# Moving cache copies, a table load and buffer choices in a hybrid decoder step

## The chip, the cores and the metric

The kernel runs on one core of a Trainium2 chip. The metric is the device time of one execution in microseconds (us); the time before is the median of three runs. The engines are named as in the profile: PE is TensorE (its matmuls; PEld its weight loads), DVE is VectorE, ACT is ScalarE, POOL is GpSimd and SP is SyncE. Each engine works through its own list of instructions in order, and transfers (DMAs) are issued from the lists of POOL and SP. "L936" is line 936 of the kernel before.

## The reference

One layer of a decoder is computed for 512 prompt tokens and for 8 samples of 4 tokens each, 544 columns in all. Cut to what matters:

```python
# mixer, for prompt and samples alike
q_a, k_a, v_a, r_a, z_a, q_b, k_b, v_b = split(rmsnorm(h) @ w_in)        # 2048 -> 6160
o_a, state = gla_recurrence(q_a, k_a, v_a, gate(z_a), state_gla)         # 10 heads, linear attention
o_a = rmsnorm(o_a) * silu(r_a)
o_b = dilated_attention(rope(q_b), concat(k_hist, rope(k_b)), concat(v_hist, v_b))   # 12 heads
h = h + concat(o_a, o_b) @ w_out
k_sample, v_sample = k_all[:, -1024:], v_all[:, -1024:]                  # the caches, moved on by 4 rows
# ConvFFN
up = rmsnorm(h) @ w_up                                                   # 2048 -> 2 x 5504
u, g = conv_b + causal_conv3(concat(conv_state, up), conv_w)
h = h + (silu(g) * u) @ w_down
y = rmsnorm(h)
```

Outputs are `y`, the linear-attention states, the new caches of the samples (1020 old rows and 4 new ones for each sample, for keys and for values) and the new convolution states.

## The kernel before

Activations stand with features on the 128 partitions and the 544 tokens along them, in two halves of 272 columns. Every large product is made of three matmuls in a reduced format: the high part of the weights with the high and the low part of the activations, and the low part of the weights with the high part. A weight unit is 8 x 128 rows by 128 columns, 512 KB: SP loads it into `raw` (three buffers), ACT writes its rounded high part `whi` (L190), and DVE the rest, `wlo` (L191), with three buffers each. A framework orders the instructions of each engine when the kernel is built, by its own estimates of time and by priorities (weight units are put far ahead), and adds the semaphores. A pool of buffers that takes over the memory of earlier pools waits until all of them are released.

The stages, in order: the q, k, v products of attention and its scores (to about 480 us); five blocks of linear attention, t = 0 to 4, each for two heads (`gla`, called at L818; the decay products E, KB, QB at L662 to L669, the scores on PE at L673), beside the input products that are left (to about 843 us); the output projection `w_out`, 16 tiles (loop from L928, to about 1061 us); the up-projection with convolution, 43 pairs of tiles (class Pair, to about 1985 us); the down-projection, first the three kept tiles (KEPT), then three groups (to the end).

What the change touches:

- **The caches' copies.** Sixteen copies (8 samples, keys and values; `kept_rows`), each from DRAM to DRAM and 3060 KB, issued on POOL's queue by `keep_rows` (L634). `keep_in_program_order` pins each behind the POOL instruction that the code issues before it. Two are issued in each block of linear attention, behind the store of the prompt's state (L738) and behind that of the samples' state (L773): ten. The other six are issued in the w_out loop at odd tiles (L945).
- **The split outputs.** Behind linear attention the 16 outputs `o` are split into high and low parts `ah`, `al` in the order 10 to 15, 0 to 9 (L869). Output k takes the pair of buffers k (`act_pair(k)`), which before held tile k of the normed input, read by the last input product.
- **The entry to the up-projection.** The pool FP opens when the pool HX of the w_out loop is closed. From it come the table `vcv` of the convolution's factors (172 KB, L1086) and the old convolution states `ci` (64 KB for four pairs, L1101), both loaded by POOL. ACT puts `ci` into the tiles F (L1028), later splits weights (L190) and copies a product from PSUM to `V` (L1038), and PE's next product into that PSUM buffer waits for this copy. The new states are gathered in `co`.
- **w_out.** For each tile POOL loads the old residual `h` from `xT` (L935), DVE adds the product (L936), and the sum is stored to `hscr` (L937).
- **Down-projection.** During the kept products, NSLOT = 11 tiles of the FFN's activations are fetched (`fetch`, SP into `ar`, two buffers, then split to `dh`, `dl`); the pool DS2 has 24 - NSLOT more. In the first group the stored residual is loaded into `hr`, one buffer of its own (L1201).

Of the kernel before, what the change touches and what calls it, by code (L numbers as in the profile page):

```python
# [9 lines left out]
F32 = mybir.dt.float32  # L10
# [7 lines left out]
P = 128  # L18
# [3 lines left out]
NB = 8  # L22
TS = 4
NS = NB * TS
NT = TP + NS
# [10 lines left out]
KF = FF // P  # L36
# [6 lines left out]
GATES_FIRST = 4  # L43
POOL_SPLIT = 6
NKEPT = 3
NSLOT = 11
FW = 2 + TP + NB * (2 + TS)


# [59 lines left out]
V_MIX, V_FFN, V_FIN, V_BG, V_GN, V_CW, V_CB = 0, 16, 32, 48, 53, 54, 54 + 258  # L109
NVEC = 54 + 258 + 86  # L110
# [13 lines left out]
def _build(tc, nc, es, xT, st_gla, ck, cv, conv_in, vecs, w_in, w_gu, w_out, w_up, w_dn,  # L124
# [123 lines left out]
    def act_pair(k):  # L248
        return (acts.tile([P, NT], F32R, tag=f"ah{k}", name=f"ah{k}"),
                acts.tile([P, NT], F32R, tag=f"al{k}", name=f"al{k}"))  # L250
# [378 lines left out]
    kept_rows = [(b, src, dst) for b in range(NB) for src, dst in ((ck, k_s), (cv, v_s))]  # L629

    def keep_rows():

        b, src, dst = kept_rows.pop(0)
        tc.keep_in_program_order(nc.gpsimd.dma_start(dst[b, 0:PAST - TS, :], src[b, TS:PAST, :]))  # L634
# [169 lines left out]
    for t in range(GP):  # L804
        q = scaled(in_tile(C_QA + t * P), "q", 0.125)
        k = scaled(in_tile(C_KA + t * P), "k")
        V = GL.tile([P, 4, 2 * P], F32, tag="V", name="V", bufs=2)
        Vs = GL.tile([NS, 2 * P], F32, tag="Vs", name="Vs", bufs=2)
        for e in range(2):
            v = scaled(in_tile(C_VA + (2 * t + e) * P), "v")  # L810
            pst = vps()
            for c in range(4):
                nc.tensor.transpose(pst[:, c * P:(c + 1) * P], v[:, c * P:(c + 1) * P], ident)
            nc.scalar.activation(V[:, :, e * P:(e + 1) * P], pst.rearrange("p (c v) -> p c v", c=4), AF.Copy)
            pst = vps()
            nc.tensor.transpose(pst[:NS, :P], v[:, TP:], ident)
            nc.scalar.activation(Vs[:, e * P:(e + 1) * P], pst[:NS, :P], AF.Copy)
        gla(t, q, k, V, Vs)  # L818
    for h in range(GATES_FIRST, 2 * GP):
        r = scaled(in_tile(C_RA + h * P), "r", -1.0)  # L820
        silu_neg(r)
        nc.vector.tensor_mul(o[h], o[h], r)
# [4 lines left out]
    wu_p, wu = opened(name="wu", bufs=1, side="right")  # L827
# [38 lines left out]

    order = [10, 11, 12, 13, 14, 15, 0, 1, 2, 3, 4, 5, 6, 7, 8, 9]
    og = [None] * KD
    for k in order:  # L869
        og[k] = act_pair(k)  # L870
        split(og[k][0], og[k][1], o[k])
    closed(rb2, rowsB_p, rowsA_p)

# [21 lines left out]
    def factors(some, X, pool):  # L895
# [24 lines left out]
        for i in some:  # L920
# [3 lines left out]
            else:  # L924
                parts(i, T3, 2, b[i][:, 1:3])

    X = {}
    for ot in range(KD):  # L928
        ps = gps()
        gemm(ps, [wpart(w_out, order[:8], ot * P), wpart(w_out, order[8:], ot * P)], og)  # L930
        i, j = divmod(ot, 2)
        if j == 0:
            hp = HX.tile([P, 2, NT], F32, tag="h", name="h", bufs=KD // 2 + 1 - AHEAD)
        ht = hp[:, j]
        nc.gpsimd.dma_start(ht, xT[ot * P:(ot + 1) * P, :])  # L935
        nc.vector.tensor_add(hv(ht), hv(ht), ps[:, :, :HT])  # L936
        nc.gpsimd.dma_start(hscr[ot], ht)  # L937
        if ot == 0:
            nc.scalar.activation(acc2, ht, AF.Square)
        else:  # L940
            sq = htmp("sq")
            nc.scalar.activation(sq, ht, AF.Square)
            nc.vector.tensor_add(acc2, acc2, sq)
        X[i] = hp
        if ot % 2 == 1 and kept_rows:  # L945
            keep_rows()
        nc.scalar.activation(ht, ht, AF.Copy, scale=vec[:, V_FFN + ot:V_FFN + ot + 1])
        if j == 1 and i < AHEAD:
            factors([i], X, VA)
# [27 lines left out]
    class Pair:  # L977
# [79 lines left out]
        def conv(self):  # L1057
            out = []
            for s, F in ((0, self.Fu), (1, self.Fg)):
# [19 lines left out]
    fp_p, FP = opened(name="ffn", bufs=1, side="right")  # L1079
# [2 lines left out]
    nc.scalar.activation(rstdF[:, 2:2 + TP], rstd[:, :TP], AF.Copy)  # L1082
    nc.scalar.activation(rstdF[:, 2 + TP:].rearrange("p (b s) -> p b s", s=2 + TS)[:, :, 2:],
                         rstd[:, TP:].rearrange("p (b t) -> p b t", t=TS), AF.Copy)
    vcv = FP.tile([P, NVEC - V_CW], F32, name="vcv")
    nc.gpsimd.dma_start(vcv, vecs[:, V_CW:])  # L1086

    ci_v = conv_in.rearrange("p (s f) r -> p s f r", s=2)
    co_v = conv_out.rearrange("p (s f) r -> p s f r", s=2)
    def sv(x):  # L1090
        return x[:, 2 + TP:].rearrange("p (b s) -> p b s", s=2 + TS)[:, :, :TS]

    KEPT = list(range(KF - 1 - NKEPT, KF - 1))
    kept = {}
    ci = co = None
    for f, pr in enumerate(pairs):
        if f % 4 == 0:
            n = min(4, KF - f)
            ci = FP.tile([P, 2, 4, 2 * NB], F32, tag="ci", name="ci", bufs=2)
            co = FP.tile([P, 2, 4, 2 + 2 * NB], F32, tag="co", name="co", bufs=2)  # L1100
            nc.gpsimd.dma_start(ci[:, :, :n, :], ci_v[:, :, f:f + n, :])  # L1101
        pr.ci, pr.co = ci[:, :, f % 4, :], co[:, :, f % 4, :]
        if f:
            pr.p5()
        pr.p6()
        pr.p2()
        pr.p7()
        if f + 1 < KF:
            pairs[f + 1].p1()
        pr.p3()  # L1110
        pr.p4()
        cu, cg = pr.conv()
        nc.scalar.activation(cg[:, :FW - 2], cg[:, :FW - 2], AF.Silu)
        a = FP.tile([P, NT], F32, tag="a", name="a", bufs=1)
        nc.vector.tensor_mul(a[:, :TP], cu[:, :TP], cg[:, :TP])
        nc.vector.tensor_mul(a[:, TP:].rearrange("p (b t) -> p b t", t=TS), sv(cu), sv(cg))
        if f in KEPT:
            kept[f] = (G0.tile([P, NT], F32R, tag="dh", name="dh"), G0.tile([P, NT], F32R, tag="dl", name="dl"))
            split(kept[f][0], kept[f][1], a)
        else:  # L1120
            nc.gpsimd.dma_start(adr[f], a)
        if f % 4 == 3 or f == KF - 1:
            f4 = f - f % 4
            nc.gpsimd.dma_start(co_v[:, :, f4:f + 1, :], co[:, :, :f + 1 - f4, :])
# [3 lines left out]
    rows_p, rows = opened(name="rows", bufs=KD)  # L1128
    ds_p, DS = opened(name="ds", bufs=NSLOT)

# [18 lines left out]
    with tc.high_priority(offset=min(1500, tc.cur_priority - P0)):  # L1149
        for k in groups[0][:NSLOT]:  # L1150
            A1[k] = fetch(k, 0)
# [7 lines left out]
    w3_p, W3 = opened(name="w3", bufs=1, side="right")  # L1159
# [8 lines left out]
    def ctile(name):  # L1168
        return W3.tile([P, NT], F32, tag="c", name=name, bufs=2)
# [20 lines left out]
    for gi, ks in enumerate(groups):  # L1190
        A = {}
        with tc.high_priority(offset=min(2000, tc.cur_priority - P0)):
            for k in ks:
                A[k] = A1[k] if k in A1 else fetch(k, where[k])
        if gi < len(groups) - 1:
            for ot in range(KD):
                ps = gps()
                gemm(ps, [wpart(w_dn, ks[i:i + 8], ot * P) for i in range(0, len(ks), 8)], A)
                nc.vector.tensor_add(hv(h[ot]), hv(h[ot]), ps[:, :, :HT])
                if gi == 0:  # L1200
                    x = W3.tile([P, NT], F32, tag="hr", name="hr", bufs=1)  # L1201
                    nc.sync.dma_start(x, hscr[ot])
                    nc.vector.tensor_add(h[ot], h[ot], x)

# [117 lines left out]
```

## Time and profile before

| | |
|---|---|
| runs of the kernel before | 2522.66, 2524.89, 2529.08 us |
| median | 2524.89 us |
| profiled execution, its own time | 2525.1 us |
| its span in the profile | 2523.3 us |
| mean granted clock of PE | 0.991 of full |
| busy, share of the span | PE 98%, DVE 64%, ACT 43%, POOL 17% |

The rows below come from this one profiled execution; its times count from the start of the span. A row of a timeline gives the start and the length of an instruction or a run of like ones; what stands in brackets is the idle time of its engine before it and what ended that. The granted clock is told in shares of full speed (2.4 GHz).

### The profile page before, as it was taken

Reading aid. Unit: us, or ns where it says so; the run is one execution under the profiler, and the core shown is the slowest. Engines: PE = TensorE matmul, PEld = TensorE weight load, DVE = VectorE, ACT = ScalarE, POOL = GpSimd, SP = SyncE. Lnnn points to the kernel's source line nnn. Section 1 sums busy time; section 2 is a strip of 40 time slices with the busy share of each in tenths; the row PEclk is TensorE's granted clock in tenths of the full one; section 3 lists DMA queues with packets and bytes.
Section 4 is the critical chain, followed back from the end, with each engine's and each line's share of the span. In section 5 each row is a group of like instructions: output and inputs, shape, how many; then the busy total and the mean of one; then the engine's idle time right before and its main releaser. Section 6 shows DMA issues by size and latency. Waiting matters only on the chain.

```text
span 2523.3 us, 47163 instructions
## 1 busy us (share of the span) xinstructions
PE 2462.7 (98%) x19479; PEld 2385.2 (95%) x19479; DVE 1619.3 (64%) x2460; ACT 1078.8 (43%) x1870; POOL 435.3 (17%) x581
## 2 busy tenths in 40 slices
PE   8999999999999899989999999999999999999997
PEld 8988887899999899989999999999999999999997
DVE  7777764267777843478878888888888643342243
ACT  6344464133334433355555555555555531131142
POOL 1333434210002320112212221222121000000001
PEclk9999999999999999999999999999999999999999
DMA  7777744544555498668888888889888473443232
GB/s 220 197 202 197 193 114 138 161 131 141 166 177 177 159 305 256 169 146 192 192 188 192 191 191 189 191 191 192 189 191 178 124 219 107 115 151 92 85 100 72
DMA packets 581593, 427.73 MB, mean 170 GB/s; under 512 B 18976, under 2 KB 553728, under 8 KB 580608
## 3 DMA queue, kind: packets, MB, share of 16 engines
q1 hardware_dynamic: 462144, 248.31, 34.9%
q0 software_dynamic: 115200, 171.02, 30.1%
q10 hardware_dynamic: 4032, 5.38, 0.6%
q8 instruction: 153, 2.51, 0.4%
q14 instruction: 64, 0.52, 0.1%
HBM read 397.40 MB, written 77.37 MB: 188 GB/s over the span
## 4 chain that ended last, share of the span: by engine, by line
PE 82%; DMA 8%; DVE 6%; issue 2%; POOL 1%; ACT 1%; SPq 0%; DVEq 0%; POOLq 0%; ACTq 0%
PE g L225 40%; PE b L965 20%; PE g L965 15%; DMA q<-qscr 6%; DVE pr L411 1%; PE v L507 1%; PE s L673 1%; DMA ar<-adr 1%; DVE wlo L191 1%; DVE kv L412 1%; PE s L561 1%; DMA xr<-in_xT_dram 0%; PE s L548 0%; PE s L795 0%; POOL q L408 0%
## 5 line engine op out<-in xcount | busy, mean ns | idle before, releaser
L191 DVE TENSOR_TENSOR wlo<-raw,whi 128x1024 fp32r<-128x1024 f32 (+1 forms) x341 | 408.3, 1198 | 295.6 <-ACT whi L190 288.7
L190 ACT ACTIVATE whi<-raw 128x1024 fp32r<-128x1024 f32 (+1 forms) x345 | 355.0, 1030 | 555.1 <-PE g L225 454.0
L225 PE MATMUL g<-ah,whi 128*128 128x272 f32 x2048 | 442.9, 296 | 9.8 <-ACT ah L190 4.6
L225 PE MATMUL g<-al,whi 128*128 128x272 f32 x2048 | 447.2, 297 | 0.5 <-DVE al L191 0.5
L225 PE MATMUL g<-ah,wlo 128*128 128x272 f32 x2048 | 442.4, 295 | 0.3 <-DVE wlo L191 0.3
L965 PE MATMUL b<-vh,whi 128*128 128x272 f32 x1376 | 395.1, 288 | 6.2 <-ACT V L1038 4.8
L965 PE MATMUL b<-vl,whi 128*128 128x272 f32 x1376 | 395.9, 289 | 0.8 <-DVE vl L893 0.6
L965 PE MATMUL b<-vh,wlo 128*128 128x272 f32 x1376 | 389.9, 288 | 1.3 <-DVE wlo L191 1.3
L225 PEld LDWEIGHTS g<-ah,whi 128*128 128x128 f32 x2048 | 327.9, 191 | 19.7 <-issue 10.3
L225 PEld LDWEIGHTS g<-al,whi 128*128 128x128 f32 x2048 | 329.2, 191 | 11.6 <-issue 9.3
L225 PEld LDWEIGHTS g<-ah,wlo 128*128 128x128 f32 x2048 | 328.3, 190 | 10.2 <-issue 8.5
L965 PE MATMUL g<-vl,whi 128*128 128x272 f32 x1032 | 298.8, 290 | 2.0 <-DVE vl L893 1.9
L965 PE MATMUL g<-vh,whi 128*128 128x272 f32 x1032 | 297.8, 289 | 0.4 <-ACT vh L892 0.3
L965 PE MATMUL g<-vh,wlo 128*128 128x272 f32 x1032 | 296.8, 288 | 0.0
L965 PEld LDWEIGHTS b<-vh,whi 128*128 128x128 f32 x1376 | 260.0, 189 | 6.7 <-ACT V L1038 5.1
L225 PE MATMUL g<-dh,whi 128*128 128x272 f32 x1248 | 258.0, 288 | 4.1 <-ACT whi L190 2.7
L965 PEld LDWEIGHTS b<-vl,whi 128*128 128x128 f32 x1376 | 259.5, 189 | 1.5 <-DVE vl L893 1.5
L965 PEld LDWEIGHTS b<-vh,wlo 128*128 128x128 f32 x1376 | 257.4, 189 | 1.5 <-DVE wlo L191 1.5
L225 PE MATMUL g<-dh,wlo 128*128 128x272 f32 x1248 | 258.2, 288 | 0.0
L225 PE MATMUL g<-dl,whi 128*128 128x272 f32 x1248 | 258.1, 288 | 0.0
L190 ACT ACTIVATE whi<-rs 128x1024 fp32r<-128x1024 f32 x129 | 136.8, 1061 | 266.8 <-PE g L965 201.1
L225 PEld LDWEIGHTS g<-dh,whi 128*128 128x128 f32 x1248 | 195.7, 188 | 5.4 <-ACT whi L190 3.4
(341 smaller groups left out, 4101.5 us busy)
## 6 DMA issues: line engine op xcount, KB each, us to landing
raw<-in_w_up_dram SPq DMA_DIRECT2D x129, 512.0 KB, 4.1
raw<-in_w_in_dram SPq DMA_DIRECT2D x96, 512.0 KB, 4.8
raw<-in_w_dn_dram SPq DMA_DIRECT2D x64, 512.0 KB, 4.0
out_k_s_dram<-in_ck_dram POOLq DMA_DIRECT2D x8, 3060.0 KB, 12.7
out_v_s_dram<-in_cv_dram POOLq DMA_DIRECT2D x8, 3060.0 KB, 14.5
ra<-in_w_up_dram SPq DMA_DIRECT2D x43, 512.0 KB, 7.9
rs<-in_w_up_dram SPq DMA_DIRECT2D x43, 512.0 KB, 3.8
rs<-in_w_up_dram POOLq DMA_DIRECT2D x43, 512.0 KB, 9.8
```

The lines of the kernel that those rows point to most:

```text
L190: nc.scalar.activation(hi, src, AF.Copy)
L191: eng.tensor_sub(lo, src, hi.bitcast(F32))
L225: nc.tensor.matmul(ps[:, s, :HT], a, b[:, s * HT:(s + 1) * HT], start=(i == 0 and n == 0), stop=(i == len(todo) - 1 and n == 2))
L411: nc.vector.tensor_mul(pr, kt[:, 4:5, :].broadcast_to([P, TS, QC]), q5[:, 1:5, :])
L412: nc.vector.tensor_mul(kt[:, 0:4, :], kt[:, 0:4, :], q5[:, 0:1, :].broadcast_to([P, 4, QC]))
L507: nc.tensor.matmul(psv[32 * m:32 * m + 32, :QC], lhs, rhs, start=(kt == 0), stop=(kt == 5), tile_position=(0, 32 * m))
L561: nc.tensor.matmul(psc[r, :P], vt[:, j * P + 64 * e:j * P + 64 * e + 64], t[:, j * P:(j + 1) * P], start=(j == 0), stop=(j == qi))
L673: nc.tensor.matmul(ps[:, c * P:(c + 1) * P], KS[:, c * P:(c + 1) * P], Q[:, :, c * 64:(c + 1) * 64], start=True, stop=True)
L965: nc.tensor.matmul(b[:, :HT], a_[:, i, :], x_[i][:, v, :], start=(first and i == 0 and n == 0), stop=(i == 7 and n == 2), skip_group_check ...
```

## The change

It has four parts.

1. `keep_rows()` is called a third time per block, after `gla(t)`. With that, 15 of the 16 copies are issued beside linear attention and the last at tile 0 of the w_out loop, where the condition on odd tiles is dropped.
2. The split outputs take the buffer pairs by their place in the order, `act_pair(n)`: output 10 the first pair, output 9 the last.
3. `vcv` and the buffers `ci` and `co` come from the pool `wu`, which opens before the w_out loop, instead of FP. `vcv` and the first `ci` are loaded by POOL before that loop; the later `ci` where they were. `wu` is 3552 bytes a partition larger.
4. NSLOT is 10 instead of 11 (so DS2 has 14 pairs instead of 13), and `hr` is taken from the two rotating buffers "c" of the down-projection.

```diff
--- before.py
+++ after.py
@@ -43,7 +43,7 @@
 GATES_FIRST = 4
 POOL_SPLIT = 6
 NKEPT = 3
-NSLOT = 11
+NSLOT = 10
 FW = 2 + TP + NB * (2 + TS)
 
 
@@ -816,6 +816,7 @@
             nc.tensor.transpose(pst[:NS, :P], v[:, TP:], ident)
             nc.scalar.activation(Vs[:, e * P:(e + 1) * P], pst[:NS, :P], AF.Copy)
         gla(t, q, k, V, Vs)
+        keep_rows()
     for h in range(GATES_FIRST, 2 * GP):
         r = scaled(in_tile(C_RA + h * P), "r", -1.0)
         silu_neg(r)
@@ -866,8 +867,8 @@
 
     order = [10, 11, 12, 13, 14, 15, 0, 1, 2, 3, 4, 5, 6, 7, 8, 9]
     og = [None] * KD
-    for k in order:
-        og[k] = act_pair(k)
+    for n, k in enumerate(order):
+        og[k] = act_pair(n)
         split(og[k][0], og[k][1], o[k])
     closed(rb2, rowsB_p, rowsA_p)
 
@@ -924,6 +925,21 @@
             else:
                 parts(i, T3, 2, b[i][:, 1:3])
 
+    vcv = wu.tile([P, NVEC - V_CW], F32, name="vcv")
+    nc.gpsimd.dma_start(vcv, vecs[:, V_CW:])
+    ci_v = conv_in.rearrange("p (s f) r -> p s f r", s=2)
+    co_v = conv_out.rearrange("p (s f) r -> p s f r", s=2)
+
+    def states(f):
+
+        n = min(4, KF - f)
+        ci = wu.tile([P, 2, 4, 2 * NB], F32, tag="ci", name="ci", bufs=2)
+        co = wu.tile([P, 2, 4, 2 + 2 * NB], F32, tag="co", name="co", bufs=2)
+        nc.gpsimd.dma_start(ci[:, :, :n, :], ci_v[:, :, f:f + n, :])
+        return ci, co
+
+    state = states(0)
+
     X = {}
     for ot in range(KD):
         ps = gps()
@@ -942,7 +958,7 @@
             nc.scalar.activation(sq, ht, AF.Square)
             nc.vector.tensor_add(acc2, acc2, sq)
         X[i] = hp
-        if ot % 2 == 1 and kept_rows:
+        if kept_rows:
             keep_rows()
         nc.scalar.activation(ht, ht, AF.Copy, scale=vec[:, V_FFN + ot:V_FFN + ot + 1])
         if j == 1 and i < AHEAD:
@@ -1082,23 +1098,15 @@
     nc.scalar.activation(rstdF[:, 2:2 + TP], rstd[:, :TP], AF.Copy)
     nc.scalar.activation(rstdF[:, 2 + TP:].rearrange("p (b s) -> p b s", s=2 + TS)[:, :, 2:],
                          rstd[:, TP:].rearrange("p (b t) -> p b t", t=TS), AF.Copy)
-    vcv = FP.tile([P, NVEC - V_CW], F32, name="vcv")
-    nc.gpsimd.dma_start(vcv, vecs[:, V_CW:])
-
-    ci_v = conv_in.rearrange("p (s f) r -> p s f r", s=2)
-    co_v = conv_out.rearrange("p (s f) r -> p s f r", s=2)
+
     def sv(x):
         return x[:, 2 + TP:].rearrange("p (b s) -> p b s", s=2 + TS)[:, :, :TS]
 
     KEPT = list(range(KF - 1 - NKEPT, KF - 1))
     kept = {}
-    ci = co = None
     for f, pr in enumerate(pairs):
         if f % 4 == 0:
-            n = min(4, KF - f)
-            ci = FP.tile([P, 2, 4, 2 * NB], F32, tag="ci", name="ci", bufs=2)
-            co = FP.tile([P, 2, 4, 2 + 2 * NB], F32, tag="co", name="co", bufs=2)
-            nc.gpsimd.dma_start(ci[:, :, :n, :], ci_v[:, :, f:f + n, :])
+            ci, co = states(f) if f else state
         pr.ci, pr.co = ci[:, :, f % 4, :], co[:, :, f % 4, :]
         if f:
             pr.p5()
@@ -1198,7 +1206,7 @@
                 gemm(ps, [wpart(w_dn, ks[i:i + 8], ot * P) for i in range(0, len(ks), 8)], A)
                 nc.vector.tensor_add(hv(h[ot]), hv(h[ot]), ps[:, :, :HT])
                 if gi == 0:
-                    x = W3.tile([P, NT], F32, tag="hr", name="hr", bufs=1)
+                    x = ctile("hr")
                     nc.sync.dma_start(x, hscr[ot])
                     nc.vector.tensor_add(h[ot], h[ot], x)
 
```

## Rows read from the trace of the kernel before

**Rows 1.** Windows: us, busy us of PE, PEld, DVE, ACT, POOL; PE clock, DMA, GB/s.

```profile
700.00:780.00 80.00, 80.00 (x672) 75.45 (x672) 56.92 (x104) 30.12 (x50) 9.39 (x10) 1.00 0.56 177
780.00:880.00 100.00, 93.84 (x734) 87.53 (x732) 84.03 (x135) 50.99 (x87) 30.64 (x20) 0.98 0.52 168
800.00:820.00 20.00, 20.00 (x164) 19.98 (x163) 19.75 (x37) 10.95 (x16) 5.52 (x3) 1.00 0.19 54
880.00:1060.00 180.00, 175.30 (x1358) 175.11 (x1358) 75.13 (x100) 60.48 (x81) 23.51 (x39) 0.97 0.81 245
...
870.00:880.00 10.00, 7.01 (x53) 6.39 (x51) 7.18 (x14) 4.34 (x9) 0.00 (x0) 0.94 0.99 345
...
1096.00:1101.00 5.00, 4.88 (x22) 4.56 (x22) 3.58 (x6) 1.21 (x4) 0.00 (x0) 0.53 1.19 209
2040.00:2480.00 440.00, 440.00 (x3518) 440.00 (x3517) 159.10 (x185) 114.78 (x139) 0.00 (x0) 1.00 0.38 111
```

**Rows 2.** Waits of PE, whole run: waited for, us in total, times, longest us.

```profile
PE b L965 <- ACT V L1038: 4.8, 1, 4.8
PE g L225 <- ACT ah L190: 4.6, 1, 4.6
```

**Rows 3.** Timeline of ACT and PE at the entry to the up-projection.

```profile
1089.02 0.21 ACT L1083 ACTIVATE rstdF<-rstd 128x32 f32<-128x32 f32 x1
1094.00 0.32 ACT L1028 ACTIVATE F<-ci 128x16 f32<-128x16 f32 x2 [4.77 <-DMA ci<-in_conv_in_dram]
...
1095.17 0.38 ACT L1038 ACTIVATE V<-b 128x272 f32<-128x272 f32 x1
...
1095.60 0.60 PE L965 MATMUL b<-vh,whi 128*128 128x272 f32 x1 [4.85 <-ACT V L1038]
```

**Rows 4.** Timeline of the DMA issues of POOL and SP.

```profile
777.40 0.54 POOL L634 DMA_DIRECT2D out_v_s_dram<-in_cv_dram  x1
...
778.65 0.37 SPq L209 DMA_DIRECT2D raw<-in_w_in_dram  x1
...
865.65 0.54 POOL L634 DMA_DIRECT2D out_v_s_dram<-in_cv_dram  x1
883.48 4.31 POOL L935 DMA_DIRECT2D h<-in_xT_dram  x8 [17.29 <-issue]
...
1088.35 0.59 POOL L1086 DMA_DIRECT2D vcv<-in_vecs_dram  x1 [2.01 <-DVE rstd L171]
1088.92 0.73 POOL L1101 DMA_DIRECT2D ci<-in_conv_in_dram  x1
```

**Rows 5.** Timeline of PE at the entry to w_out.

```profile
889.82 0.79 PE L225 MATMUL g<-ah,whi 128*128 128x272 f32 x2 [3.14 <-DVE h L936]
```

**Rows 6.** DMAs issued at 655, 777, 778 and 883 us: KB, us to landing.

```profile
raw<-in_w_in_dram SPq DMA_DIRECT2D x1, 512.0 KB, 4.1
...
out_v_s_dram<-in_cv_dram POOLq DMA_DIRECT2D x1, 3060.0 KB, 15.9
...
raw<-in_w_in_dram SPq DMA_DIRECT2D x1, 512.0 KB, 18.0
...
h<-in_xT_dram POOLq DMA_DIRECT2D x1, 272.0 KB, 5.4
```

**Rows 7.** The page's groups: busy us, mean ns, idle before them.

```profile
L225 PE MATMUL g<-al,whi 128*128 128x272 f32 x2048 | 447.2, 297 | 0.5 <-DVE al L191 0.5
```

**Rows 8.** Timeline of ACT behind the kept products.

```profile
2023.81 0.66 ACT L190 ACTIVATE dh<-ar 128x544 fp32r<-128x544 f32 x1 [1.28 <-DMA ar<-adr]
```

**Rows 9.** Timeline of ACT, DVE and PE in linear attention's last block.

```profile
800.38 1.06 ACT L190 ACTIVATE whi<-raw 128x1024 fp32r<-128x1024 f32 x1 [1.66 <-PE g L225]
801.47 1.44 DVE L191 TENSOR_TENSOR wlo<-raw,whi 128x1024 fp32r<-128x1024 f32 x1
...
810.08 0.85 DVE L669 TENSOR_TENSOR QB<-q,E 64x256 f32<-64x256 f32 x2
810.10 2.04 PE L673 MATMUL s<-QB,KB 128*128 128x128 f32 x16
```

## The prediction, made before the change was run

> **What bounds the kernel now.** The windows by stage come first: TensorE (PE) is busy for all of 80 us beside linear attention, for 440 of 440 us in the down-projection, and loses time in few places: 6.2 us in 780 to 880 us and 4.7 us in 880 to 1060 us [rows 1]. So an edit pays only if it shortens one of PE's own gaps, and costs only if it opens a new one. PE's waits come second: the longest is 4.8 us on V (L1038), then 4.6 us on ah [rows 2]. The instructions around those gaps come third. In the first, ACT is done at 1089.23 us (1089.02 plus 0.21), sits 4.77 us for the conv state `ci`, and only then reaches V, on which PE waits 4.85 us [rows 3]; `ci` was issued as late as 1088.92 us, behind the table `vcv` on POOL's queue [rows 4]. The second and third lie at the start of w_out: PE waits 4.6 us for the last split of the linear-attention outputs [rows 2] and, up to 889.82 us, 3.14 us for `h` [rows 5], whose load POOL issued at 883.48 us [rows 4], with 5.4 us to landing [rows 6]. After a gap PE doesn't run at the full 2.4 GHz at once: in 1096 to 1101 us the granted clock is 0.53, half, and 22 matmuls start in 5 us [rows 1]. At full clock one starts every 440/3518 = 0.125 us, so 22 take 2.75 us, and 2.2 us are lost beside the gap itself.
>
> **The early table and conv state.** Issued before the w_out loop, `vcv` and `ci` land some 200 us before ACT asks. ACT then does its L1028 at 1089.2 us, the weight split behind it, and V as soon as its product ends on PE, 1095.60 - 4.85 = 1090.75 us. V's start to PE's restart is 1095.60 - 1095.17 = 0.43 us [rows 3], so PE goes on at about 1091.4 us with some 0.2 us for the order on ACT: 4.2 us saved, and with so short a gap the 2.2 us of half clock too, **-6.4 us**. Bounds: -4 us if the half clock stays, -7.5 us if the rest of the gap goes as well. The two loads now stand on POOL's queue ahead of the `h` load. They cost it 0.59 and 0.73 us of issue [rows 4], but POOL idles 17.29 us before that load [rows 4], so they lie under that idle time; if POOL could not start them before 883.48 us, `h` would come 1.3 us later. The larger `wu` pool (3552 bytes a partition) moves no work; it is paid for below.
>
> **The freed buffers.** The split outputs now take activation buffers in the order in which the last input product frees them. PE's own waits on `al` in the whole run are 0.5 us [rows 7], and the 4.6 us gap ends with the split `ah` of the last linear-attention outputs, which are late because their values are [rows 2]: a buffer that is free earlier doesn't bring them. I take **-0.5 us**, bounds +3 us (another order of splits on DVE) and -3 us.
>
> **Room.** Ten slots instead of eleven: the eleventh prefetched tile is split on ACT at 2023.81 us after a wait for its own `ar` load [rows 8], behind the kept products, and the stage after it keeps PE at 440 of 440 us [rows 1]. `hr` goes into a rotating pair of buffers with two tenants instead of one of its own; the add that needs it is on DVE, busy for 159 of 440 us there [rows 1]. **0**, bounds -2 and +2 us.
>
> **Copies leave w_out.** PE's lost 4.7 us in 880 to 1060 us are the 3.14 us gap and the tail of the one before it [rows 1, 2, 5]; behind them it is always busy although five more copies run there. Taking those out gives PE nothing: **0**. Bounds: 0, and -1 us for a shorter tail of the half clock.
>
> **Copies beside linear attention.** This is the part that decides. Each copy is 3060 KB [rows 6]. While one runs, DMA is 0.99 busy at 345 GB/s (870 to 880 us) [rows 1], so it takes 3060/345 = 9 us in which there is no room. A copy issued at 777.40 us lands after 15.9 us, at 793.3 us, and the weight load issued at 778.65 us takes 18.0 us, landing at 796.65 us; away from a copy one takes 4.1 us [rows 4, 6]. A weight load beside a copy thus waits until the copy is through. The third copy of a block is pinned on POOL behind the second, with nothing of POOL between, so it is issued about 0.55 us after it and runs directly behind. The weight load then lands 9 us later.
>
> The Trainium skill, "DMA: Bandwidth & Descriptors", the paragraph on arbitration, says that a DMA engine alternates between the queues that have work and drains a whole packet of one before it turns to the next; that speaks against this change, since copies with long packets would take most of the time whatever stands in the other queue. The trace agrees as far as 18.0 us beside a copy against 4.1 us without go [rows 6]. Were the two served by bytes instead, the load would land early, and the sum would be that of the second case below.
>
> What the 9 us do differs by block. In blocks 0 to 2 (the stretch 700 to 780 us stands for them) DVE is busy 56.92 of 80 us and PE idles nowhere, beside two copies [rows 1]: a weight part that is late by a few us is made up. I take **+1 us** for the three, bounds 0 and +6 us. The third copy behind block 3 (at 777.95 us) meets the start of block 4. The load landing at 796.65 us is split at 800.38 us, so 3.7 us of lateness are free; with its landing at 805.7 us the split is 5.3 us late, and `wlo`, at 801.47 us on DVE, with it [rows 9]. Behind `wlo` DVE has the decay products up to QB at 810.08 us, with DVE busy 19.75 of 20 us [rows 1], so nothing is made up; PE starts the scores from QB within 0.02 us of QB's start [rows 9], so it stands still some 5.2 us, and 2.2 us of half clock follow: **+7.4 us**. Bounds: 0, if the loads issued ahead are split in another order or PE has products to put in, and +10 us.
>
> Block 4's own third copy is issued at 865.65 + 0.55 = 866.2 us [rows 4] and runs when the second is through, to about 889 us. The `h` load is behind it on POOL's queue: 883.48 + 5.4 = 888.9 us becomes between 890 (272 KB at 345 GB/s, behind 889) and 894.6 us [rows 4, 6]. I take 892.4: **+3.5 us** on the 3.14 us gap, bounds 0 (if the queue serves both side by side) and +5.7 us.
>
> **Sum.** -6.4 - 0.5 + 0 + 0 + 1 + 7.4 + 3.5 = +5.0 us. The profiled run took 2525.1 us (its span 2523.3); 2530.1 us follows. The median of the runs shown is 0.2 us below the profiled one, so **2530 us** stands for both.
>
> **Rivals.** *Absorbed*: block 4 doesn't feel the copy behind block 3, because other loads stand ready in three raw buffers. For it: PE is at 80 of 80 us with two copies a block. Against it: DVE's 19.75 of 20 us. -6.4 - 0.5 + 1 + 3.5 = -2.4 us, 2523 us. *No harm at all*: also the `h` load isn't held. Against it: both go through one queue. -6.4 - 0.5 = -6.9 us, 2518 us; with both edits at their better bounds 2515 us. *Slower than before*: blocks 0 to 2 stall as block 4 does. It decides where a weight load is late by more than the few us for which a loaded split waits. Two of the three blocks at 3 to 4 us beyond the slack make +7 instead of +1 us: +11 us, 2536 us. For it: the next load behind a copy is late too, since the copies of a block now fill 27 us in place of 18. *The table changes nothing*: V waits for something else at 1089 us. The rows show ACT with no other cause than `ci` [rows 3], so I give it no chance of its own; it would add 6.4 us to each case.
>
> **How the numbers follow.** The forecast 0.45, absorbed 0.28, no harm 0.15, slower 0.12. A measurement tells 0.3% (7.6 us) from no change: faster is below 2517.3 us, slower above 2532.5 us. Faster holds about half of no harm and a little of absorbed, 0.09. Slower holds all of the slower case and about a third of the forecast (its block 4 and `h` terms at their upper bounds give +10 us), 0.27. The rest, 0.64, is within. The forecast's own range is 2523 to 2535 us; for 8 in 10 the range goes from 2516 to 2537 us.
>
> **What would show it.** Right: PE's wait on V near 1090 us falls from 4.8 us to under 1 us and the clock there stays full; weight loads issued in the 10 us behind block 3 take some 27 us; PE waits about 5 us before the scores of block 4, and above 5 us for `h` in w_out. Wrong: the loads land in 18 us or less with three copies, or the gap at 810 us isn't there (absorbed); the wait on `h` stays at 3 us (no harm); waits on whi or wlo in the blocks before the last (slower). What breaks all cases alike is another order of instructions around w_out's start, for the order is made from estimated times, which the moved loads and buffers change.

## The result: slower, and by more than the range allowed

The changed kernel takes 2542.77 us (median of four runs, 2540.99 to 2547.64) against 2525.61 us before (median of four runs too), a ratio of 1.0068 (95% interval 1.0056 to 1.0080). That is 17 us more; the forecast was 2530 us, and the range ended at 2537 us. The profiled run has a span of 2539.2 us, 15.9 us above the one before.

PE does the same 19479 matmuls in both kernels, so the place of the lost time can be read by counting: the start of the n-th matmul, from the first one on, in the two traces.

```
matmul no.   start before, us   later after by, us   what lies between the rows
  4251            558.9                 +0.9         start, attention, block 0
  4501            592.1                 +7.0         entry of block 1
  6001            771.9                 +7.5         blocks 1 to 3
  6651            857.6                +13.3         block 4
  7001            915.1                +16.9         entry of w_out
  8001           1040.7                +16.9         w_out
  8501           1121.6                +11.2         entry to the up-projection
 15501           1998.0                +15.8         up-projection
 15751           2035.8                +13.9         kept products
 19479           2504.0                +16.3         down-projection
```

In the first row the third copies have done nothing yet; there the traces of the runs below lie between -2.3 and +1.3 us of the one before, so a difference of under 2 us between two traces is no reading by itself.

Four things stand out: two stalls of about 6 us (blocks 1 and 4), 3.6 us at w_out's entry, the gain of 5.7 us at the entry to the up-projection, and a loss of 4.6 us that grows evenly through a stage in which PE waits for nothing.

PE's waits in the changed kernel, the counterpart of [rows 2] (what PE waited for, us in total, times, longest us):

```profile
PE g L225 <- DVE h L952: 8.8, 1, 8.8
PE s L673 <- DVE QB L669: 8.3, 3, 5.1
...
PE g L225 <- ACT ah L190: 4.8, 1, 4.8
...
PE v L816 <- ACT V L814: 3.3, 1, 3.3
...
PE b L981 <- ACT V L1054: 0.8, 1, 0.8
```

The wait on V has fallen from 4.8 to 0.8 us, as meant. The wait on h has grown from 3.1 to 8.8 us, and the two waits before scores and transposes of linear attention (QB, V of L814) are longer or new (before: 2.2 us in one wait for QB, none for V of L814).

**The entry of block 1**, timelines of ACT, DVE and PE of the changed kernel:

```profile
584.03 0.66 ACT L646 ACTIVATE l<-l 128x544 f32<-128x544 f32 x1
593.05 1.06 ACT L190 ACTIVATE whi<-raw 128x1024 fp32r<-128x1024 f32 x1 [8.36 <-DMA raw<-in_w_in_dram]
594.01 0.64 ACT L647 ACTIVATE l<-l 128x544 f32<-128x544 f32 x1
...
594.14 1.23 DVE L191 TENSOR_TENSOR wlo<-raw,whi 128x1024 fp32r<-128x1024 f32 x1 [8.57 <-ACT whi L190]
595.28 0.72 DVE L648 TENSOR_TENSOR l<-l,l 128x544 f32<-128x544 f32 x1
...
595.19 0.28 PE L816 MATMUL v<-small,v 128*32 128x128 f32 x1 [3.31 <-ACT V L814]
601.95 2.38 PE L673 MATMUL s<-QB,KB 128*128 128x128 f32 x16 [2.09 <-DVE QB L669]
```

ACT sits for 8.36 us in front of a weight split whose load hasn't landed, and DVE for 8.57 us behind it. The next steps of the decay chain (L647 on ACT, L648 on DVE) don't need these weights; they only stand behind the split. The load was issued at 559.84 us, between the first of block 0's copies and the other two, and landed 33.1 us later, behind the last of them (589.8 us).

**The entry of block 4** has the same form, at the place that the prediction named (landing of the load issued at 786.18 us, then the timelines; [rows 9] before):

```profile
raw<-in_w_in_dram SPq DMA_DIRECT2D x1, 512.0 KB, 28.6
...
814.86 1.06 ACT L190 ACTIVATE whi<-raw 128x1024 fp32r<-128x1024 f32 x1 [8.35 <-DMA raw<-in_w_in_dram]
...
815.95 1.23 DVE L191 TENSOR_TENSOR wlo<-raw,whi 128x1024 fp32r<-128x1024 f32 x1 [6.75 <-ACT whi L190]
...
822.84 3.48 PE L673 MATMUL s<-QB,KB 128*128 128x128 f32 x16 [5.07 <-DVE QB L669]
```

**The entry of w_out**, POOL's issues and PE ([rows 4, 5] before):

```profile
881.24 0.53 POOL L634 DMA_DIRECT2D out_k_s_dram<-in_ck_dram  x1
894.81 0.60 POOL L929 DMA_DIRECT2D vcv<-in_vecs_dram  x1 [13.04 <-DVE oa L823]
895.41 1.45 POOL L938 DMA_DIRECT2D ci<-in_conv_in_dram  x2
896.86 2.15 POOL L951 DMA_DIRECT2D h<-in_xT_dram  x4
...
907.98 0.79 PE L225 MATMUL g<-ah,whi 128*128 128x272 f32 x2 [8.78 <-DVE h L952]
```

The table's load isn't free under POOL's idle time. It starts 0.3 us behind the end of the last L823, and the h load 2.35 us behind it; in the kernel before, that load starts 2.0 us behind the same instruction (L822 there, ended at 881.46 us). So by its issue the table delays h by little; but copy, table, states and h land one behind the other on POOL's queue: the third copy at 905.0 us, `vcv` at 905.6, the last `ci` at 906.2 and the first h at 907.0 us.

**The up-projection.** A window of 800 us in which PE never idles, before (1130 to 1930 us) and after (1150 to 1950 us), with the columns of [rows 1]; first the kernel before:

```profile
1130.00:1930.00 800.00, 800.00 (x6398) 800.00 (x6397) 640.86 (x878) 411.68 (x722) 161.85 (x209) 1.00 0.89 191
```

and the changed kernel:

```profile
1150.00:1950.00 800.00, 800.00 (x6364) 800.00 (x6363) 639.44 (x872) 410.37 (x721) 160.19 (x209) 1.00 0.88 190
```

Same clock, same busy time, 34 matmuls fewer: 125.71 ns a matmul instead of 125.04 ns, 0.53%. (A window also counts matmuls that only reach into it; from start to start, over matmuls 9001 to 15001, it is 125.75 and 125.08 ns.)

### The profile page after: what moved, and what is told of

The parts are those of the page before. It is cut to its first block, busy times and chain, and to the rows that moved or that the text cites. A ratio compares the mean times of both kernels' runs of the same rounds, so it can differ in the third digit from the quotient of the medians.

```text
span 2539.2 us, 47150 instructions
## 1 busy us (share of the span) xinstructions
PE 2463.5 (97%) x19479; PEld 2387.0 (94%) x19479; DVE 1617.7 (64%) x2460; ACT 1078.4 (42%) x1870; POOL 436.7 (17%) x581
## 4 chain that ended last, share of the span: by engine, by line
PE 76%; DMA 12%; DVE 6%; issue 4%; POOL 1%; ACT 1%; SPq 0%; DVEq 0%; ACTq 0%; POOLq 0%
PE g L225 36%; PE b L981 20%; PE g L981 15%; DMA q<-qscr 6%; DMA raw<-in_w_in_dram 3%; DVE pr L411 1%; PE v L507 1%; DVE wlo L191 1%; DMA ar<-adr 1%; PE s L561 1%; DVE kv L412 1%; PE s L673 0%; DMA xr<-in_xT_dram 0%; PE s L548 0%; ACT whi L190 0%
## 5 line engine op out<-in xcount | busy, mean ns | idle before, releaser
L225 PE MATMUL g<-ah,whi 128*128 128x272 f32 x2048 | 440.8, 294 | 15.9 <-DVE h L952 8.8
```

What stands on the lines that cost most here:

```text
L225: nc.tensor.matmul(ps[:, s, :HT], a, b[:, s * HT:(s + 1) * HT], start=(i == 0 and n == 0), stop=(i == len(todo) - 1 and n == 2))
```

## The experiments

Theory after the result: the third copies hold back weight loads and with them the decay chains, and the last one holds h; the new tiles move the operands of the later stages to addresses at which each matmul is a little slower. Rivals: the copies cost everything, the evenly growing loss among it; or the freed buffers or the smaller room do.

**Each part alone.** First the copies alone on the kernel before:

```diff
         gla(t, q, k, V, Vs)
+        keep_rows()
...
-        if ot % 2 == 1 and kept_rows:
+        if kept_rows:
             keep_rows()
```

> The kernel before with the third copy per block alone (15 copies beside linear attention, one left in w_out). Theory 1 (the rise is the copies': weight loads behind three copies in a row hold up the decay chains): the stalls near 595 and 820 us (about 6 us each) and the longer wait on h in w_out (about 4 us) all return, TensorE's wait on V stays at 4.8 us: 2525 + 16 = 2541 us, and the matmuls of the up-projection keep 125.1 ns from start to start. Theory 2 (the copies cost only part, about 10 us, and something in the placement of the moved buffers costs the rest): 2535 us or less. Theory 3 (the slower matmuls of the later stages come with the copies, since these end earlier or later): 2548 us, with 125.7 ns between matmuls.

2539.18 us against 2523.72 us, ratio 1.0061 (1.0046 to 1.0076). By the count of matmuls it is level up to block 4, +7 us there, +6.7 us more at w_out's entry, and constant from then on: +13.2 us at the end, with the spacing in the up-projection as before. Block 1 doesn't stall here, and the wait on h is longer than in the changed kernel, without a table ahead of it:

```profile
PE g L225 <- DVE h L937: 10.3, 1, 10.3
```

So the copies cost 13 us (by the traces) to 15.5 us (by the medians) by themselves, and the evenly growing loss isn't theirs. Theory 3 falls, and so does theory 2, by which the copies cost only 10 us. Theory 1 has the total (2541 us) but not its parts: the stall near 595 us is missing, and the wait on h is longer in its place.

Then the changed kernel without its third copies (the same edit undone; copies at odd tiles of w_out again):

> The changed kernel without its third copies: freed buffers, early table and smaller room alone, copies as before. Theory 1 (the rise is the copies' alone): 2525 - 6 = 2519 us, wait on V near 1 us, 125.1 ns between matmuls in the up-projection. Theory 2 (the moved buffers slow each later matmul by some 0.5%, about 7 us in all): 2525 - 6 + 7 = 2526 us with 125.7 ns between matmuls, no stall near 595 us.

2525.48 us, ratio 1.0005 (0.9996 to 1.0014): no change, with no stall near 595 us, 3.7 us ahead after the entry to the up-projection and behind again at the end. That is theory 2's number. With the 15.5 us of the copies alone, the 1.8 us by which this run lies above the kernel before make up the changed kernel's 17.2 us.

The same with the buffers of the split outputs as before:

```diff
-    for n, k in enumerate(order):
-        og[k] = act_pair(n)
+    for k in order:
+        og[k] = act_pair(k)
```

> Early table and smaller room, with the buffers of the split outputs as before and the copies as before. If the freed buffers are worth nothing, the same as the run without third copies within 1 us; if they bring forward or disturb the entry to w_out, the two differ there (before the first w_out product) by up to 3 us. Placement theory: 125.7 ns between matmuls here too; otherwise 125.1 ns.

2524.13 us, ratio 1.0001 (0.9992 to 1.0011). The freed buffers thus cost about 1 us, if anything: the ranges of the two runs overlap (2523.16 to 2526.66 and 2521.70 to 2526.83 us), and by the count of matmuls the run with freed buffers, 1.4 us behind the other from before block 1 on, is 3.0 us behind at the end of block 4 (matmul 6651), where the order of instructions differs, and 2.2 us in w_out: 0.8 us that stay, no more than two traces differ by chance. At the entry to the up-projection it loses 1.5 us more (it gains 4.2 us there, the other 5.7); the changed kernel has the freed buffers too and gains 5.7 us, so that isn't put down to them. PE's wait on h is 4.4 us in the run with the table only, against 3.1 us before: 1.3 us for the table ahead of h.

The smaller room alone (NSLOT 10, `hr` from the pair "c"):

> Ten prefetched tiles instead of eleven and hr in the rotating pair, nothing else. The working put it at 0, bounds -2 and +2 us: 2523 to 2527 us. If the slower matmuls of the down-projection come from the placement of its tiles, they show here in the down-projection alone (about +2 us); if they come from the table's place, they don't.

2524.80 us, ratio 1.0003 (0.9994 to 1.0012): nothing in sum, as forecast. In the down-projection alone the matmuls are slower, 125.52 ns from start to start (matmuls 16001 to 19001) instead of 125.14 ns, which is 1.3 us behind the kept products.

**The addresses.** The table's tile is made 32 bytes longer, with no instruction changed, so that the tiles below it lie 3584 bytes lower than in the kernel before, a multiple of 512, instead of 3552. Three variants: on the table-only kernel,

```diff
-    vcv = wu.tile([P, NVEC - V_CW], F32, name="vcv")
-    nc.gpsimd.dma_start(vcv, vecs[:, V_CW:])
+    vcv = wu.tile([P, NVEC - V_CW + 8], F32, name="vcv")
+    nc.gpsimd.dma_start(vcv[:, :NVEC - V_CW], vecs[:, V_CW:])
```

> Early table and room as in the run with the table only, with the table's tile 32 bytes longer, so that the activations of the up-projection that lie below it start 32 bytes off a multiple of 64, as in the kernel before; the instructions are the same. Placement theory (the start address of the operands that TensorE streams sets the time of a matmul): 125.1 ns between matmuls in the up-projection instead of 125.75, some 4.5 us less, and up to 2.5 us in the down-projection: 2518 to 2520 us. If the larger pool slows the matmuls in another way (its size, or the traffic of the table's readers): 125.75 ns again and 2524 us.

2519.23 us, ratio 0.9985 (0.9976 to 0.9994). The same window of 800 us, with the table only and then with the padded table:

```profile
1150.00:1950.00 800.00, 800.00 (x6364) 800.00 (x6363) 638.47 (x873) 410.16 (x720) 160.88 (x206) 1.00 0.88 189
```

```profile
1150.00:1950.00 800.00, 800.00 (x6398) 800.00 (x6398) 641.33 (x878) 413.40 (x725) 161.14 (x209) 1.00 0.88 190
```

The 34 matmuls are back: 32 bytes of padding are worth 4.9 us by the medians, 4.6 us by the count of matmuls in the up-projection. On the changed kernel itself:

> The changed kernel with the table's tile 32 bytes longer and nothing else, so the instructions are the same and only the start addresses of the tiles below it move. If the placement of the streamed operands is part of the changed kernel's rise: matmuls of the up-projection at 125.08 ns, of the down-projection at 125.52 ns as with the padded table, and 5 to 6 us less than the changed kernel: 2537 us. If the rise is the copies' alone: 2542 us.

2535.25 us, ratio 1.0043 (1.0027 to 1.0058), with 6398 matmuls in the window. That is 11.7 us above the kernel before as measured beside it (2523.56 us), where the changed kernel was 17.2 us above: 5.5 us less, as expected. 4.6 us of it are the up-projection; the stall in block 1 is also shorter in this trace (1.76 and 2.08 us instead of 3.31 and 2.09 us). And with a further 32 bytes ahead of the tiles at the other end of the memory:

```diff
-    eps = cons.tile([P, 1], F32, name="eps")
+    eps = cons.tile([P, 9], F32, name="eps")[:, :1]
```

> As the padded table, with 32 bytes more ahead of the activations of the input products and of w_out, so that nearly all streamed operands start 32 bytes off a multiple of 64. Placement theory: w_out's matmuls also go from 125.56 to about 125.1 ns, and the input products and the second half of the up-projection's operands with them: 2514 to 2518 us. If an odd start only helped by chance of the mix of both: no better than the padded table, 2519 us, or worse.

2519.31 us: no further gain in sum. By the count of matmuls the up-projection and the down-projection gain (124.88 and 125.05 ns from start to start, against 125.08 and 125.52 ns with the padded table), w_out is unchanged at 125.56 ns, and the input products lose (126.02 ns instead of 125.38 ns over matmuls 300 to 480). So "32 bytes off" isn't a rule: the same shift helps one stage and hurts another.

Across all runs the spacing goes by the placement alone, with or without third copies: in the up-projection 125.75 ns in the six kernels with the unpadded early table, 125.08 ns in the six with the table's old place or with its padding, 124.88 ns in the two in which the operands of its second half are shifted too. The weight parts `whi` and `wlo` come from a pool (`wts`) that by the code none of these edits moves, which leaves the activations among PE's operands; no run separates them further.

**The copies.** A third copy behind blocks 1 and 2 only, on the kernel before:

```diff
         gla(t, q, k, V, Vs)
+        if t in (1, 2):
+            keep_rows()
```

> The kernel before with a third copy behind blocks 1 and 2 only, four copies left in w_out. Theory (a third copy costs only where the split of the late weights stands ahead of a decay chain that TensorE waits for, behind blocks 0 and 3, and ahead of w_out's h load, behind block 4): 2524 us, the same as before. If any third copy costs some 4 us: 2532 us.

2531.46 us, ratio 1.0038 (1.0023 to 1.0053): a miss. Behind block 1 the copy costs nothing; behind block 2 it costs 7.9 us by the count of matmuls at the entry of block 3, where the copies-only run and the changed kernel lose nothing behind the same three copies:

```profile
736.59 0.40 PE L816 MATMUL v<-small,v 128*32 128x128 f32 x1 [6.27 <-ACT V L814]
```

The load behind it, issued 0.3 us after block 2's first copy, lands after 35.5 us; in the copies-only run, also issued 0.3 us after it, after 13.5 us. Any block can stall, and which one does isn't read from the issue times; what decided it is shown below.

Without the third copy behind block 4, the rest of the change kept:

```diff
         gla(t, q, k, V, Vs)
-        keep_rows()
+        if t < GP - 1:
+            keep_rows()
```

> The changed kernel without the third copy behind block 4 (14 copies beside linear attention, two in w_out). If the longer wait on w_out's first h is that copy's: the wait falls from 8.8 us to 3 to 4.5 us and the time by 4 to 5 us, to 2538 us. If the h load is late for another reason (the table's issue ahead of it): the wait stays above 8 us and 2542 us.

2535.86 us (2533.64 to 2538.55), 12.3 us above the kernel before as measured beside it instead of 17.2, and the wait on h is halved:

```profile
902.81 0.48 PE L225 MATMUL g<-ah,whi 128*128 128x272 f32 x2 [4.65 <-DVE h L953]
```

8.8 to 4.65 us; what is left above 3.1 us is the table ahead of h, as in the run with the table only (4.4 us). By the count of matmuls w_out's entry now costs nothing (-0.4 us instead of +3.6).

**What holds the loads.** The DMA packets in 579 to 582 us of the changed kernel, when block 0's copies run and the load of block 1 is outstanding (q0 carries POOL's copies, q1 SP's loads; packets, MB, share of the DMA engines):

```profile
q0 software_dynamic: 17, 0.98, 106.9%
q1 hardware_dynamic: 17, 0.01, 1.0%
```

One packet of a load for one of a copy, but the copy's hold 58 KB on average (0.98 MB over 17; the built program describes a copy as 48 pieces of 16320 numbers, 65,280 bytes) and the load's some 500 bytes, as the next window shows (0.76 MB over 1504). In the same window of the kernel before the second copy is through, and the loads have the DMAs to themselves:

```profile
q1 hardware_dynamic: 1504, 0.76, 100.0%
q0 software_dynamic: 37, 0.09, 12.0%
```

Where only the rest of an older load is left, the share is smaller still: from 571 to 577 us of the changed kernel 32 packets of POOL's queue went against 2 of SP's.

This also shows which load stalls. A load of 512 KB is 1040 packets (counted in 549.9 to 554.3 us of the kernel before, where one ran without a copy). Of a load issued behind the first copy nearly all packets pass in a gap of some 4 us between that copy and the next two; one that isn't through by then lands only behind the last copy. The load of block 1's entry from its issue to the end of the gap (560 to 571 us), in the changed kernel and then with the copies alone:

```profile
q1 hardware_dynamic: 987, 0.50, 18.7%
```

```profile
q1 hardware_dynamic: 1038, 0.52, 17.8%
```

The first lands after 33.1 us, behind the last copy, and block 1 stalls; the second lands after 17.0 us, and it doesn't. Two more runs have the stall, with 983 (padded table) and 1009 packets (no copy behind block 4). At block 2's end it is the same: the load that landed after 35.5 us, 0.6 us behind the last copy, had at most 1001 packets through by 712 us, the one that landed after 13.5 us all 1040. Some tens of packets thus decide over 4 to 8 us.

To test whether a copy's long pieces are what holds the loads, the copies were described in shorter ones. A first try gave each copy two outer halves:

```diff
-        ... dst[b, 0:PAST - TS, :], src[b, TS:PAST, :]
+        ... dst[b, 0:PAST - TS, :].rearrange("s (x d) -> x s d", x=2),
+            src[b, TS:PAST, :].rearrange("s (x d) -> x s d", x=2)
```

> The changed kernel with every cache copy described in pieces of 1536 bytes (half a row) instead of long contiguous ones; the same bytes. If the long packets of a copy are what holds the weight loads back (a queue gives way only between packets), the loads beside three copies land within 15 us or less, the stall near 820 us goes, w_out's wait on h may stay: about 2542 - 8 = 2534 us. If it is the bandwidth alone that the copies fill, the loads stay at 23 to 28 us and the time at 2541 us. If the copies themselves become much slower in pieces, they reach into w_out and past it: slower than 2543 us.

3418.67 us: each copy now takes 67 to 75 us to land, and POOL, whose later issues wait for it, falls behind, PE with it. Nothing about the packets can be read from this run; it shows only that with an outer dimension of two a copy runs at some 46 GB/s (3060 KB in 67.7 us, the median of the key copies). The second try issues two DMAs per copy, of 1020 rows each:

```diff
-        tc.keep_in_program_order(nc.gpsimd.dma_start(dst[b, 0:PAST - TS, :], src[b, TS:PAST, :]))
+        for x in (slice(0, DW // 2), slice(DW // 2, DW)):
+            tc.keep_in_program_order(nc.gpsimd.dma_start(dst[b, 0:PAST - TS, x], src[b, TS:PAST, x]))
```

> The changed kernel with each cache copy issued as two, one for the left and one for the right half of every row, so that it is described in pieces of 1536 bytes over 1020 rows, and not in 48 pieces of 65,280 bytes. If weight loads are late because each DMA engine gives them only one short packet per long piece of a copy: loads beside copies land within 15 us, the stalls before the decay chains go: 2542 - 7 to 12 us, 2530 to 2536 us. If what counts is the bandwidth that is taken: unchanged, 2542 us. If the pieces make the copies slower than the gaps allow: above 2545 us.

2530.78 us (2527.35 to 2531.95), ratio 1.0025 (1.0015 to 1.0034): 7.2 us above the kernel before instead of 17.2, with the same bytes copied at the same places. The window 579 to 582 us again, now with pieces of 1536 bytes (a packet of q0 holds 4.4 KB on average, 0.79 MB over 178):

```profile
q0 software_dynamic: 178, 0.79, 86.2%
q1 hardware_dynamic: 179, 0.09, 10.3%
```

Still one for one in this window, but ten times as many turns. The load of block 1's entry lands after 16.9 us instead of 33.1, the one ahead of block 4 after 20.9 instead of 28.6 us (not within 15, as expected), and both stalls are gone: the kernel is level at matmul 6001 (-0.2 us) and +1.0 us at 6651. The second is the stronger evidence, for with long pieces that load landed after 28.6 and 28.8 us (copies alone), while block 1's got through after 17.0 us with the copies alone. Here 1007 of its packets had passed by 570 us, and the rest landed at 575.7 us, among the copies and not behind them (590.4 us). The wait on h stays at 8.8 us: h is behind the copy in POOL's own queue, whatever the pieces.

**A faster version.** Copies and split outputs as before, the early table with its padding, 32 bytes ahead of the tiles of the second half of the up-projection's operands and of the down-projection's, and the table issued at tile 8 of w_out:

```diff
+    VB.tile([P, 8], F32, name="odd")
...
+        if ot == 8:
+            tc.keep_in_program_order(nc.gpsimd.dma_start(vcv[:, :NVEC - V_CW], vecs[:, V_CW:]))
+            state = states(0)
...
+    rows.tile([P, 8], F32, tag="odd", name="odd", bufs=1)
```

> Copies and split outputs as before; the early table with the 32 bytes, 32 bytes more ahead of the second half of the up-projection's operands and of the down-projection's tiles, and the table and first states issued at tile 8 of w_out instead of ahead of its h load. Expected from the two padded runs: 2519.2 us, less 1.4 us (up-projection at 124.88 ns), less 1.9 us (down-projection at 125.05 ns), less 1 us (wait on h back at 3.1 us): 2515 us. If the order of loads or the second pad is worth nothing: 2519 us.

2514.45 us (2512.34 to 2516.42) against 2523.56 us, ratio 0.9964 (0.9951 to 0.9976). The wait on h is 2.6 us, and the window shows an up-projection as fast as with both ends padded (6409 matmuls there):

```profile
1150.00:1950.00 800.00, 800.00 (x6408) 800.00 (x6407) 640.66 (x878) 414.17 (x726) 162.38 (x209) 1.00 0.88 190
```

## Why the prediction was wrong, step by step

- **Early table, -6.4 us: right in size.** 5.7 us at the entry to the up-projection (16.9 to 11.2 us late), the wait on V 0.8 us, the clock full behind it (1.00 in 1104 to 1112 us). That the wait on V was PE's longest [rows 2] is not so: one of 6.3 us, for wz (L341), stands in both kernels, and the change doesn't touch it.
- **"The larger pool moves no work": this step failed.** It moves no work, but it moves the operands. 4.6 us in the up-projection are the address effect, shown by the padding; the gain of the table is given back within the next stage. In the down-projection the changed kernel loses another 2.4 us behind the kept products (125.79 ns from start to start instead of 125.14). The smaller room alone takes 1.3 us there (125.52 ns), and so does the changed kernel with the padded table, 1.2 us (125.52 ns): the room has about half of it, the table's place the rest. No row before could show this, since the effect needs two placements to be seen.
- **Room, 0, and copies leaving w_out, 0: right in sum.** 2524.80 us with the room alone, inside its bounds, though for the room not because nothing changed: 1.3 us are lost in the down-projection. w_out is 16.9 us late at both ends.
- **Freed buffers, -0.5 us (bounds -3 and +3): no gain seen, the bounds hold.** They change the order in block 4; the medians of two overlapping runs differ by 1.4 us, their traces by 0.8 us up to w_out. That isn't clear of zero.
- **Blocks 0 to 2, +1 us (bounds 0 and +6): this step failed.** Block 1 costs 6.1 us, just past the bound. The reasoning was that DVE, busy 56.92 of 80 us [rows 1], would make up for a late weight part. It can't, because the idle time lies in front of the late split: the lists of ACT and DVE are fixed, the decay chain stands behind the split, and both engines idle for over 8 us with work at hand. The rival "slower than before" had this, with +7 us and a chance of 0.12. Its reason names the next load behind a copy; the one that was late here was issued between the first copy and the second, and missed the gap by 53 of its 1040 packets. So where a stall falls is partly luck: the copies alone stall at block 4 but not at block 1.
- **Block 4, +7.4 us: right place and mechanism.** 5.07 us of wait at QB; by the count of matmuls the step is 5.8 us, with the freed buffers' other order in it. The load issued behind the three copies took 28.6 us (some 27 forecast).
- **h in w_out, +3.5 us: right in mechanism, at the upper bound in size.** The wait went from 3.14 to 8.78 us, 5.6 us more (bound +5.7), 4.1 of them the copy's by the run without it and 1.5 us the table's. The table was put under POOL's idle time of 17.29 us, but it could start only about 2 us ahead of h, and h then lands behind it on the queue. The split holds for this order alone: the copies alone make the wait 7.2 us longer, past the bound. The net loss is 3.6 us by the count of matmuls.

The sum was +5.0 us, the trace shows +16.3. By the count of matmuls the 11.3 us between them are 5.6 us in blocks 1 to 3, 5.1 us behind the entry to the up-projection (4.6 in it, 2.4 in the down-projection, -1.9 at the kept products, which wasn't forecast and wasn't followed up), 0.9 us in the start and attention (within what traces differ by there), 0.7 us of the table, and -1.1 us at block 4 with the freed buffers. The median lies 1.8 us above the profiled run.

The Trainium skill, "DMA: Bandwidth & Descriptors", the paragraph on arbitration, says that an engine goes round its queues and drains a packet of one before it takes the next. In 579 to 582 us the 17 packets against 17, and 179 against 178 with short pieces, agree, as far as a sum over 16 engines can: turns are shared evenly there, bytes are not.

What stays open: why the last packets of a load that missed the gap pass so slowly (2 against 32 in 571 to 577 us), since no view here gives the packets by DMA engine. And the exact rule for the addresses: an operand 32 bytes off helps the up- and the down-projection and hurts the input products.

## What to carry to other kernels

A stage whose bound engine is always busy gained nothing when background copies left it, and a stage with in-order chains paid when they came: ask which instruction stands behind the one that waits for the delayed load, not how idle the engine is. Large background copies are better issued in short pieces (here 7.2 us above the kernel before instead of 17.2), or with gaps between them that are long enough for the small loads (here a gap missed by tens of packets cost 4 to 8 us). After any change to the pools, compare the number of matmuls in a long window without idle time: a shift of 32 bytes was worth 4.6 us here, about as much as the wait that the change set out to remove (4.85 us).

## What the runs showed of the hardware

- The time of a matmul depends on where its operands lie (by the code, of these the activations). With the same instructions, clock and busy time, 800 us of the up-projection hold 6364, 6398 or 6408 matmuls (125.71, 125.04 and 124.84 ns) by placement alone; the value is the same, within one matmul, in every kernel with the same placement.
- In 579 to 582 us two queues share the DMAs packet for packet. A copy in 48 pieces of 65,280 bytes leaves the loads, in 512-byte packets, 17 packets in 3 us; in 1536-byte pieces it leaves them 179.
- Beside copies in such long pieces, a load issued behind the first passes in the gap ahead of the next two or waits for the last: with 987 of 1040 packets through at the gap's end it landed after 33.1 us, with 1038 after 17.0 us.
- A copy whose description has an outer dimension of two took 67 to 75 us for 3060 KB, where one in 48 pieces landed after 15.9 us beside another [rows 6].
